# First attention of a two-block network: sums of the query and key products' inputs on VectorE instead of GpSimd

## The chip, the cores and the metric

One core of a Trainium2 chip runs the whole program in one launch. The metric is device time in microseconds (us) of that core; lower is better. TensorE (PE) multiplies, VectorE (DVE), ScalarE (ACT) and GpSimd (POOL) work on elements, SyncE (SP), ACT and POOL issue transfers (DMAs).

## The reference

The input is one sequence of 512 tokens of 1024 channels, float32. The first block is a conformer-like mixer with a SwiGLU network and a final RMS norm. The second has two layers: a "fox" attention layer (16 heads of 64, with a forget gate) and a differential attention layer, each followed by a layer norm and a gated network with a convolution of width 3. What the change touches is the start of the fox attention:

```python
def _fox_attention(x, w_in, b_f, w_out):
    proj = x @ w_in                                  # 1024 -> 3*1024 + 16
    q = _heads(proj[..., :d], FOX_HEADS, HEAD_DIM)
    k = _heads(proj[..., d:2 * d], FOX_HEADS, HEAD_DIM)
    v = _heads(proj[..., 2 * d:3 * d], FOX_HEADS, HEAD_DIM)
    f_logit = proj[..., 3 * d:] + b_f
    c = jnp.cumsum(jax.nn.log_sigmoid(f_logit), axis=1)
    ...                                              # causal softmax(q k^T / 8 + c_q - c_k) v, then @ w_out
```

## The kernel before

Each float32 operand is split into a rounded high part and a low part (`split`, L182: ScalarE copies the high part, L183; VectorE subtracts it from the source for the low part, L185, or GpSimd does where it is asked to). A product is three matmuls, high x high, high x low and low x high (`mm3`, L433 to L438). The activations stand transposed in SBUF as `xh` and `xl`, eight blocks of 128 channels by 512 tokens. Weights come in pieces of 128x1024: SyncE loads a raw tile, ScalarE and VectorE convert it to `wh` and `wl` (`_convert`), four pieces are held at most and two are made ahead of use.

The fox layer (`fox`, L1112) begins while the last product of the network before it (`dn`) ends. VectorE adds that to the residual (L848), GpSimd makes the row's scale (a power, `rs_r`, through the helper `pool`, L176), VectorE scales the row tile (L357), TensorE transposes it (L337, tiles `pt`), and ScalarE and VectorE split it into `xh` and `xl`. This is done for four row tiles of 128 tokens. The value product `ta` (`t_phase`, L1149) starts on the first two row tiles; its two halves of 512 channels are evacuated from PSUM to `va` by `split`. Then come the small forget-gate product `pf` and the query and key products.

Query and key products use a scheme of seven block products instead of eight (`fast_chunk`, L493; PSUM tiles `c1`, `c2`). The weights' combinations are made from loaded blocks: an accumulating transfer on GpSimd's queue (L274, `raw<-raw`) and two GpSimd additions (L277, L278, also `raw<-raw`). The activations' combinations are made once, by `sums` (L465). `xh`+`xl` is taken as four quarters (channel half by token half) of 128x1024 each, then five sums and differences of them, `z`, in two buffers by turns, and each is split into high and low parts: into new tiles (`g1`, `g6`, `g7`) or in place over two quarters of `xh` and `xl`. `sums` is a generator. Its first step (four quarters and two of the five) is traced at the fifth channel block of the value product's first half, together with a spill of the residual X to DRAM; three further steps follow in the second half at blocks 1, 3 and 5, inside `behind(1)`, which orders ScalarE's and VectorE's instructions of the step behind the conversion made last; the rest is traced after the forget gate's chain:

```python
if k == 4 and not half:
    self.spill()
    ...
    next(sums)
elif half and k in (1, 3, 5):
    with self.behind(1):
        next(sums)
```

GpSimd's queue also carries, in this stretch, up to five paced steps: after a conversion a copy of one column of `wh` (L150, `paced`) and then an accumulating transfer of 704 KB for the next network's weights (L152), as well as the load of the forget gate's weights (L1153) and the store of its sums (L1172).

The order of instructions on each engine is set when the program is built: a list scheduler takes, for each engine, the ready instruction that was traced first, by its own model of time, except where a stretch is pinned (`manual_schedule`) or an order is asked for (`issue_after`). Each engine then runs its list in order. The two networks' own sums (`wide`, L788) use the same function with GpSimd and are not touched.

Of the kernel before, what the change touches and what calls it, by code (L numbers as in the profile page):

```python
# [99 lines left out]
class Net:  # L100
# [73 lines left out]
    def pool(self, *args, **kw):  # L174

        self.pooled = self.nc.gpsimd.tensor_tensor(*args, **kw)  # L176
        return self.pooled
# [284 lines left out]
                self.f_tile(ps, self.piece())  # L462
            evac(c, *pss)

    def sums(self, g, new, tmp, zs):  # L465


        A, B = slice(0, 4), slice(4, 8)
        t, u = slice(0, 256), slice(256, 512)
        here = lambda k, q: (self.xh[:, k, q], self.xl[:, k, q])  # L470
        gp = self.pool
        for x, (k, q) in zip(tmp, ((A, t), (A, u), (B, t), (B, u))):
            h, l = here(k, q)
            gp(x, h.bitcast(F32), l.bitcast(F32), op=ALU.add)
        b11, b12, b21, b22 = tmp
        ops = ((b11, b22, ALU.add), (b11, b12, ALU.add), (b21, b22, ALU.add), (b21, b11, ALU.subtract), (b12, b22, ALU.subtract))
        n, z = len(zs), {}

        def add(m):
            if m < len(ops):  # L480
                z[m] = zs[m % n]()
                x, y, op = ops[m]
                gp(z[m], x, y, op=op)

        for m in range(n):
            add(m)
        g.update({2: here(A, t), 5: here(B, u), 1: new(1), 6: new(6), 7: new(7), 4: here(B, t), 3: here(A, u)})
        for m, i in enumerate((1, 6, 7, 4, 3)):
            yield
            self.split(*g[i], z[m])  # L490
            add(m + n)
# [620 lines left out]
    def fox(self):  # L1112
        nc, tc, a = self.nc, self.tc, self.a
        with ExitStack() as es:
            pool = lambda name, bufs=1: es.enter_context(tc.tile_pool(name=name, bufs=bufs))
            self.more = pool("more")
            one = pool("fox")
# [14 lines left out]

            self.fz = two
            sums, g = None, {}

            def lhs_v(k, half):
                nonlocal sums
                if k == 4 and not half:
                    self.spill()
                    f32 = lambda tag, c: two.tile([P, c], F32, name="sum", tag=tag)[:, :1024].rearrange("p (a b) -> p a b", b=256)  # L1140
                    sums = self.sums(g, self.places(one), [f32(tag, 1024) for tag in ("qh", "qh", "kh", "kh")], [partial(f32, "p", 1280)] * 2)
                    next(sums)
                elif half and k in (1, 3, 5):
                    with self.behind(1):
                        next(sums)
                return self.xh[:, k, :], self.xl[:, k, :]

            with self.mixing(1, 5):
                self.t_phase(KD, lhs_v, v_out, tail=2, head=4)  # L1149
# [40 lines left out]
            def scores(u):  # L1190
                j, e = divmod(u, 2)
                p = two.tile([P, 1280], F32, name="p", tag="p")
                for qb in range(NT):
                    n = (qb + 1) * P
                    pq = p[:, po_[qb]:po_[qb] + n]
                    sc = self.qk(qb, e, qs[j], ks[j], ib, mb)
                    nm = self.sm.tile([P, 1], F32, name="nm", tag="nm")
                    sc = sc[:, :n]
                    nc.vector.tensor_tensor_reduce(sc, sc, cbs[j][:, e, :n], 1.0, 3e38, ALU.add, ALU.min, nm)
                    sm = self.sm.tile([P, 1], F32, name="se", tag="se")  # L1200
                    nc.scalar.activation(sc, sc, AF.Exp, bias=nm, scale=-1.0, accum_out=sm)
                    r = self.sm.tile([P, 1], F32, name="re", tag="re")
                    nc.vector.reciprocal(r, sm)
                    nc.vector.tensor_scalar(pq, sc, r, None, op0=ALU.mult)
                return p
# [38 lines left out]
            p = scores(0)  # L1244
            for u in range(16):
# [7 lines left out]
                p = nxt  # L1253
# [8 lines left out]
            g, b = self.row(R_AG), self.row(R_AB)  # L1262
# [300 lines left out]
```

## Time and profile before

| | us |
|---|---|
| Timed runs, median of 3 (lowest, highest) | 1784.56 (1781.68, 1785.53) |
| Profiled execution | 1781.66 |
| its span, first to last instruction | 1779.6 |
| busy in the span: PE / DVE / ACT / POOL | 1673.8 / 1445.4 / 1008.7 / 779.9 |
| mean granted TensorE clock | 0.981 |

All times of the trace count from the first instruction. Busy time is the time in which an engine executed something; a line of a timeline gives the start, the duration, the engine, the line of the kernel, the operation with its output and inputs, and in brackets how long the engine was idle before and which instruction ended that. Where a neighbouring pair is merged, x2 stands behind it. A line number can be that of a helper: L176 is any GpSimd operation through `pool`, L185 the low part of any split. The granted clock is TensorE's, as a share of full speed (2.4 GHz).

### The profile page before, as it was taken

What the parts mean: (1) busy time and instruction counts of PE and PEld (TensorE: products, weight loads), DVE (VectorE), ACT (ScalarE), POOL (GpSimd) and SP (SyncE); (2) the same over time, 40 slices, a digit from 0 to 9 for tenths busy, and PEclk for the clock granted to TensorE, in tenths of its full rate; (3) what the DMA queues carried; (4) which work ended last, traced back from release to release, by engine and by line L of the source; (5) the groups of instructions that cost most, each with busy time, mean ns of one, the idle gap of its engine ahead of it and who ended that gap; (6) DMA issues with size and microseconds to landing.
All of it is one profiled execution on the core that took longest, in us unless ns stands there. A gap on an engine that the chain in (4) does not pass through costs nothing. (4 is left out here: it accounts for less than half of the span.)

```text
span 1779.6 us, 28078 instructions
## 1 busy us (share of the span) xinstructions
PE 1673.8 (94%) x10432; PEld 1485.5 (83%) x10432; DVE 1445.4 (81%) x2198; ACT 1008.7 (57%) x1733; POOL 779.9 (44%) x537
## 2 busy tenths in 40 slices
PE   7977999999999899989999999999888999999996
PEld 6856999998787789879999987787766789999875
DVE  6984676678885789967899899865888679988999
ACT  6662444446552678736666564654667455656563
POOL 2484643330035576217556527334332175465522
PEclk9988999999999999999999999999999999999998
DMA  6469566668967564844566689787443235666552
GB/s 232 169 186 251 152 165 185 180 179 305 342 205 201 140 175 130 222 119 135 136 190 172 176 274 347 222 227 202 113 114 97 79 108 163 179 194 184 190 183 106
DMA packets 106072, 326.05 MB, mean 183 GB/s; under 512 B 9888, under 2 KB 10016, under 8 KB 93904
## 3 DMA queue, kind: packets, MB, share of 16 engines
q1 hardware_dynamic: 73088, 215.53, 35.2%
q0 software_dynamic: 25648, 73.54, 22.1%
q10 hardware_dynamic: 7200, 35.20, 5.5%
q8 instruction: 82, 1.34, 0.3%
q14 instruction: 54, 0.44, 0.1%
HBM read 274.91 MB, written 73.43 MB: 196 GB/s over the span
## 5 line engine op out<-in xcount | busy, mean ns | idle before, releaser
L183 ACT ACTIVATE wh<-raw 128x1024 fp32r<-128x1024 f32 x457 | 450.6, 997 | 405.5 <-PE c L437 94.2
L185 DVE TENSOR_TENSOR wl<-raw,wh 128x1024 fp32r<-128x1024 f32 (+1 forms) x415 | 535.5, 1305 | 139.6 <-ACT wh L183 135.9
L176 POOL TENSOR_TENSOR raw<-raw 128x512 f32<-128x512 f32 x124 | 189.9, 1532 | 255.3 <-DMA raw<-raw 227.9
L436 PE MATMUL c<-xh,wh 128*128 128x256 f32 x992 | 284.2, 287 | 13.3 <-ACT m L519 9.0
L437 PE MATMUL c<-xl,wh 128*128 128x256 f32 x992 | 282.6, 285 | 0.0
L438 PE MATMUL c<-xh,wl 128*128 128x256 f32 x992 | 282.1, 284 | 0.0
L436 PEld LDWEIGHTS c<-xh,wh 128*128 128x128 f32 x992 | 190.8, 192 | 16.1 <-ACT m L519 11.0
L437 PEld LDWEIGHTS c<-xl,wh 128*128 128x128 f32 x992 | 190.9, 192 | 0.1
L438 PEld LDWEIGHTS c<-xh,wl 128*128 128x128 f32 x992 | 190.8, 192 | 0.0
L438 PE MATMUL dn<-wh,hl 128*128 128x512 f32 x462 | 181.7, 394 | 7.7 <-DVE hl L185 7.6
L437 PE MATMUL dn<-wl,hh 128*128 128x512 f32 x462 | 181.8, 394 | 2.5 <-DVE wl L185 2.4
L436 PE MATMUL dn<-wh,hh 128*128 128x512 f32 x462 | 179.1, 394 | 0.1
L436 PE MATMUL fa<-xh,wh 128*128 128x256 f32 (+1 forms) x400 | 133.4, 333 | 1.6 <-ACT wh L183 1.6
L437 PE MATMUL fa<-xl,wh 128*128 128x256 f32 (+1 forms) x400 | 132.8, 332 | 1.2 <-DVE xl L185 1.2
L176 POOL TENSOR_TENSOR wl<-raw,wh 128x1024 fp32r<-128x1024 f32 (+1 forms) x42 | 96.7, 2317 | 84.6 <-ACT wh L183 81.5
L438 PE MATMUL fa<-xh,wl 128*128 128x256 f32 (+1 forms) x400 | 132.6, 331 | 0.5 <-DVE wl L185 0.5
L150 POOL COPY paced<-wh 128x1 f32<-128x1 f32 x48 | 35.8, 745 | 220.1 <-ACT wh L183 220.0
L176 POOL TENSOR_TENSOR rs_r<-rs_t,mhalf 128x1 f32<-128x1 f32 (+1 forms) x40 | 32.3, 809 | 195.1 <-DVE rs_t L326 195.1
L438 PEld LDWEIGHTS dn<-wh,hl 128*128 128x128 f32 x462 | 87.7, 190 | 27.7 <-DVE hl L185 9.7
L176 POOL TENSOR_TENSOR hT<-hT,tv 128x512 f32<-128x512 f32 x44 | 93.2, 2117 | 37.5 <-DVE tv L1004 33.2
L437 PEld LDWEIGHTS dn<-wl,hh 128*128 128x128 f32 x462 | 87.6, 190 | 23.7 <-DVE wl L185 5.7
L436 PEld LDWEIGHTS dn<-wh,hh 128*128 128x128 f32 x462 | 87.8, 190 | 18.7 <-ACT wh L183 0.5
(305 smaller groups left out, 4597.6 us busy)
## 6 DMA issues: line engine op xcount, KB each, us to landing
raw<-in_w_conv_dram SPq DMA_DIRECT2D x36, 1024.0 KB, 4.9
mixed<-in_narrow_dram ACTq DMA_DIRECT2D x48, 704.0 KB, 6.3
raw<-raw POOLq DMA_DIRECT2D x62, 512.0 KB, 5.1
raw<-mixed SPq DMA_DIRECT2D x51, 512.0 KB, 6.0
raw<-in_narrow_dram SPq DMA_DIRECT2D x48, 512.0 KB, 5.5
raw<-in_w_ffn_dram SPq DMA_DIRECT2D x18, 1024.0 KB, 4.8
mixed<-in_narrow_dram POOLq DMA_DIRECT2D x24, 704.0 KB, 10.2
mixed<-mixed POOLq DMA_DIRECT2D x24, 704.0 KB, 9.6
```

Source lines behind the costliest of these rows:

```text
L150: paced = self.nc.gpsimd.tensor_copy(m, self.ready[-1][0][:, 0:1].bitcast(F32))
L176: self.pooled = self.nc.gpsimd.tensor_tensor(*args, **kw)
L183: self.copied = self.nc.scalar.activation(hi, src, AF.Copy)
L185: return self.copied, sub(lo, src, hi.bitcast(F32), op=ALU.subtract)
L436: mm(ps, lh, rh, start=first, stop=False)
L437: mm(ps, lh, rl, start=False, stop=False)
L438: mm(ps, ll, rh, start=False, stop=last)
```

## The change

`sums` takes an engine's two-operand instruction as an optional argument, and the fox layer passes VectorE's. So the four additions of `xh` and `xl` and the five sums and differences, nine instructions of 128x1024 float32, are issued on VectorE. The splits stay on ScalarE and VectorE; the two networks still use GpSimd.

```diff
-    def sums(self, g, new, tmp, zs):
+    def sums(self, g, new, tmp, zs, engine=None):
...
-        gp = self.pool
+        gp = engine or self.pool
         for x, (k, q) in zip(tmp, ((A, t), (A, u), (B, t), (B, u))):
             h, l = here(k, q)
             gp(x, h.bitcast(F32), l.bitcast(F32), op=ALU.add)
...
-                    sums = self.sums(g, self.places(one), [f32(tag, 1024) for tag in ("qh", "qh", "kh", "kh")], [partial(f32, "p", 1280)] * 2)
+                    sums = self.sums(g, self.places(one), [f32(tag, 1024) for tag in ("qh", "qh", "kh", "kh")], [partial(f32, "p", 1280)] * 2, nc.vector.tensor_tensor)
```

## Rows read from the trace of the kernel before

**Rows 1.** The page: busy us of each engine, share of the span, instructions.
```profile
PE 1673.8 (94%) x10432; PEld 1485.5 (83%) x10432; DVE 1445.4 (81%) x2198; ACT 1008.7 (57%) x1733; POOL 779.9 (44%) x537
```

**Rows 2.** Stretches: length, PE, PEld, DVE, ACT, POOL busy, clock, DMA share, GB/s.
```profile
529.00:541.00 12.00, 7.79 (x38) 5.79 (x37) 11.32 (x9) 3.64 (x6) 8.97 (x8) 1.00 0.66 198
541.00:585.00 44.00, 44.00 (x198) 33.80 (x196) 24.84 (x18) 15.57 (x22) 25.91 (x17) 1.00 0.65 162
585.00:590.00 5.00, 0.70 (x5) 0.49 (x5) 5.00 (x5) 2.60 (x4) 2.76 (x2) 1.00 0.65 111
590.00:594.00 4.00, 4.00 (x23) 3.93 (x21) 3.97 (x8) 2.04 (x3) 0.00 (x0) 0.57 0.92 315
...
625.00:760.00 135.00, 132.09 (x946) 117.36 (x944) 121.70 (x347) 102.62 (x238) 67.45 (x46) 1.00 0.65 176
```

**Rows 3.** TensorE's timeline, the four instructions that ended its longer waits.
```profile
533.13 0.50 PE L437 MATMUL ta<-wl,xh 128*128 128x512 f32 x1 [0.94 <-DVE wl L185]
...
540.80 1.07 PE L337 MATMUL pt<-ident,X 128*128 128x128 f32 x8 [3.25 <-DVE X L357]
...
589.51 0.39 PE L436 MATMUL c<-xh,wh 128*128 128x256 f32 x1 [4.29 <-DVE va L185]
...
617.47 0.58 PE L436 MATMUL c<-g1h,wh 128*128 128x256 f32 x1 [2.61 <-ACT wh L183]
```

**Rows 4.** VectorE's timeline, 529 to 591 us.
```profile
529.65 3.42 DVE L185 TENSOR_TENSOR wl<-raw,wh 128x1024 fp32r<-128x1024 f32 x1
...
534.19 2.35 DVE L185 TENSOR_TENSOR wl<-raw,wh 128x1024 fp32r<-128x1024 f32 x2
...
537.28 3.37 DVE L357 SCALAR_TENSOR_TENSOR X<-X,rs_r,row 128x1024 f32<-128x1024 f32 x1 [0.68 <-POOL rs_r L176]
...
548.45 7.21 DVE L185 TENSOR_TENSOR wl<-raw,wh 128x1024 fp32r<-128x1024 f32 x3 [0.65 <-ACT wh L183]
...
560.65 4.03 DVE L185 TENSOR_TENSOR g<-sum,g 128x1024 fp32r<-128x1024 f32 x1
578.51 1.23 DVE L185 TENSOR_TENSOR wl<-raw,wh 128x1024 fp32r<-128x1024 f32 x1 [13.84 <-ACT wh L183]
...
582.02 6.83 DVE L185 TENSOR_TENSOR wl<-raw,wh 128x1024 fp32r<-128x1024 f32 x2
588.78 2.47 DVE L185 TENSOR_TENSOR va<-ta,va 128x512 fp32r<-128x512 f32 x4
```

**Rows 5.** GpSimd's timeline, 529 to 588 us.
```profile
529.39 2.60 POOL L176 TENSOR_TENSOR sum<-xh,xl 128x1024 f32<-128x1024 f32 x1 [0.98 <-PE dn L438]
...
537.24 2.33 POOL L176 TENSOR_TENSOR sum<-xh,xl 128x1024 f32<-128x1024 f32 x1
...
547.70 5.75 POOL L176 TENSOR_TENSOR sum<-sum 128x1024 f32<-128x1024 f32 x2
553.39 1.18 POOL L150 COPY paced<-wh 128x1 f32<-128x1 f32 x1
...
580.86 3.39 POOL L176 TENSOR_TENSOR sum<-sum 128x1024 f32<-128x1024 f32 x1
...
584.99 2.77 POOL L176 TENSOR_TENSOR sum<-sum 128x1024 f32<-128x1024 f32 x1
```

**Rows 6.** Instructions on tile `sum`: ns min/median/max, first and last start.
```profile
L176 POOL TENSOR_TENSOR sum<-sum x5: 2404/2874/3390, 547.7 to 585.0; 128x1024 f32<-128x1024 f32 x5
L176 POOL TENSOR_TENSOR sum<-xh,xl x4: 2333/2389/2595, 529.4 to 545.2; 128x1024 f32<-128x1024 f32 x4
...
L185 DVE TENSOR_TENSOR xl<-sum,xh x2: 1206/1208/1210, 591.8 to 594.0; 128x1024 fp32r<-128x1024 f32 x2
```

**Rows 7.** ScalarE's timeline before the query products.
```profile
577.42 1.06 ACT L183 ACTIVATE wh<-raw 128x1024 fp32r<-128x1024 f32 x1 [17.00 <-DMA raw<-raw]
...
582.84 2.04 ACT L183 ACTIVATE va<-ta 128x512 fp32r<-128x512 f32 x4
```

**Rows 8.** Line L274, 500 to 760 us: accumulating transfers, issue to landing.
```profile
DMA to landing us min/median/max: 5.0/5.6/17.3
```

## The prediction

> **What bounds the kernel now.** I read the page first: TensorE is busy 94% of the span, VectorE 81%, GpSimd 44% [rows 1]. So an edit on VectorE or GpSimd is worth what it does to TensorE's idle time, and I look for that idle time where the nine sums stand. The table of stretches [rows 2] gives it: from 529 to 541 us TensorE works 7.79 of 12.00 us, from 541 to 585 it has no gap, from 585 to 590 it works 0.70 of 5.00 us, and from 590 to 594 it works throughout, at a granted clock of 0.57. In the long attention stretch behind (625 to 760 us) it is busy 132.09 of 135 us and VectorE 121.70; there is nothing in it for this change to gain.
>
> TensorE's own timeline names who ended each gap [rows 3]: 0.94 us for a weight half `wl` (gap a), 3.25 us for VectorE's scaled row tile `X` of L357 (gap b), 4.29 us for the evacuation `va` of the value product (gap c), and later 2.61 us for a converted weight piece (gap f). The reader is to see that a, b and c all wait for VectorE.
>
> Why VectorE was late stands in its timeline, laid beside GpSimd's [rows 4, 5]. The subtraction `wl` at 529.65 took 3.42 us and ended at 533.07; a GpSimd sum ran from 529.39 to 531.99. A pair of such subtractions with no GpSimd sum beside it took 2.35 us (at 534.19), so one takes about 1.2. The scaling at 537.28 took 3.37 us; a GpSimd sum ran from 537.24 to 539.57. The pair at 582.02 took 6.83 us, beside the sums at 580.86 (3.39 us) and 584.99 (2.77 us). Each time the VectorE instruction lasts about its own time plus what was left of the sum: the two engines take turns on such operands. So a sum on GpSimd costs VectorE twice what it would cost there, while VectorE holds what TensorE waits for.
>
> **The change, part by part.**
> *Removed from GpSimd:* nine sums of 128x1024, four of `xh`+`xl` (median 2389 ns) and five of sums (median 2874 ns), 23.9 us [rows 6].
> *Added to VectorE:* the same nine. No row shows this addition on VectorE; the nearest has the same size, the same strided blocks and both inputs in SBUF: `xl<-sum,xh`, 1206 to 1210 ns [rows 6]. I take 1.21 us each, 10.9 us in all. The lower end is the back-to-back price of half the pair at 534.19, 1.18 us; the upper, if a GpSimd instruction runs beside it, the 3.42 us of the blocked `wl`. Few GpSimd instructions are left there to do that, hence the low end.
> *Given back on VectorE:* the stalls behind sums [rows 4]. At 529.65: 3.42 - 1.2 = 2.2 us; at 537.28: 3.37 - 1.2 = 2.2; the three at 548.45: 7.21 - 3.5 = 3.7; at 560.65: 4.03 - 1.2 = 2.8; the pair at 582.02: 6.83 - 2.35 = 4.5. Together 15.4 us against 10.9 added: VectorE is 4.5 us less busy.
>
> The price that matters is that at TensorE's gaps.
> - Gap a: `wl` at 529.65 ends at 530.9 instead of 533.07, before TensorE wants it (533.13 - 0.94 = 532.2). Even with one sum of 1.21 us ahead of it it ends at 532.1. Saved: 0.94 us (0 to 0.94).
> - Gap b: without a sum beside it the scaling ends 2.2 us earlier. Everything behind the `wl` of gap a (the residual additions, ScalarE's square, the scaling) also comes up to 2.2 us earlier, and one or two of the four sums whose inputs exist by then may stand ahead of it, at 1.21 us each. These two I let cancel: 2.2 us (0.7 to 3.25).
> - Gap c: the first query product needs a PSUM buffer that `va` frees. ScalarE delivers its half at 583.4 (the first of four in 2.04 us from 582.84 [rows 7]), but VectorE's half starts at 588.78, behind the pair of 6.83 us. With 2.35 us for the pair and one sum of 1.21 ahead of it, VectorE is through with the pair at 582.0 + 3.56 = 585.6 and with its first `va` at 586.2 (a quarter of 2.47 us), if its input chain doesn't move. TensorE was free at 585.2 (589.51 - 4.29), and gaps a and b bring it there 3.1 us sooner, at 582.1. So the chain has to come sooner as well. It begins with the accumulating transfer of the first query/key block, which ScalarE awaits until 577.42 [rows 7]: 17.3 us to landing where the median is 5.6 [rows 8]. Ahead of it on the same queue are three paced weight transfers of 704 KB, which GpSimd issues from 553.39 on, once its sums of 547.70 are done [rows 5]. With the sums gone, GpSimd's queue (L150, L152, L1153, L274) moves up. By how much it lands earlier no row shows: at most 17.3 - 5.6 = 11.7 us, at the least nothing, and below nothing if the paced transfers collide with the block's own load. I take the length of the two sums ahead of them less the conversions they also wait for: an estimate of 4 us from the 5.75 us of those two [rows 5]. Then `va` is there at 582.2 and gap c closes: 4.3 us saved (0.2 if the landing stays at 577).
> - Clock: after gap c the granted clock is 0.57 for 4.00 us of full work [rows 2], which costs 4.00 x 0.43 = 1.7 us. After the 3.25 us of gap b it stayed at 1.00, so a gap of that size need not lower it. With c closed I count the 1.7 (0 to 1.7).
>
> Three of the five `z` sums stand in a new order: they are traced behind the weight conversion made last on VectorE (the `behind(1)` block), and each needs a `z` buffer that a split frees. The first two of them are ready by 564.7 (the split at 560.65 [rows 4]), and VectorE then has 13.84 us with nothing to do until 578.51, which hides them; the last follows the third split and costs its 1.21 us ahead of the pair, counted above. Queued behind these sums are weight halves and `va`; what hides them from TensorE is that it has converted pieces in hand (no gap from 541 to 585 [rows 2]). If that cover is gone, each sum costs TensorE 1.21 us.
>
> A rule that speaks against the change stands in the Trainium skill, page "Perfetto Trace Analysis", section "Optimizing Scalar/DVE Operations": the two engines share an SBUF read port, so shifting work between them might not help, and with a saturated VectorE work should rather go off it. By that the sum would be about nothing. The trace agrees on the sharing (3.42 us beside a sum, 2.35 for two without one) and not on the conclusion here, since the same sum holds the port for 2.4 to 2.9 us from one side and 1.2 from the other.
>
> Sum: 0.9 + 2.2 + 4.3 + 1.7 = 9.1 us. The profiled execution took 1781.66 us, 2.1 beyond its span, and lies 2.9 below the median of the three timed runs, 1784.56. Its time would become 1772.6; from the median, which I take as the likelier level of the next runs, 1775.5.
>
> **The rivals.**
> 1. *The forecast*, 9.1 us gained: 1775.5. For it: all three gaps end on a VectorE instruction that ran beside a sum.
> 2. *The transfer decides.* The first block still lands at 577; then `va` comes at 586.2 whatever happened before, and TensorE starts the query products there instead of at 589.51. Gained 3.3 us; the idle time before them remains about 4 us and the clock drops all the same: 1781.3. For it: 17.3 us to landing with the DMA engines full. Against: its queue moves up.
> 3. *Given back behind.* TensorE runs into the weight supply instead: gap f shows that the third block already comes 2.61 us late. If the supply to the third block keeps its time, f grows by what was gained and all behind 617 stands where it stood: 1784.6. Against: each load waits for a buffer that a VectorE `wl` frees, and these come sooner too.
> 4. *VectorE's queue.* Program order is only a wish: the sums may be put ahead of what TensorE waits for, from the first on, with none in an idle time. Then they cost 9 x 1.21 = 10.9 us, against 0.94 + 2.2 + 4.3 = 7.4 returned at the gaps: 3.5 us slower, 1788.1. It decides as soon as more than six of the nine (7.4 / 1.21) stand in TensorE's way. Against: TensorE has no gap from 541 to 585, where all but the first two start [rows 2, 5], and VectorE is idle for 13.8 us of that.
>
> **How the numbers follow.** Chances: forecast 0.60, transfer 0.13, given back 0.15, queue 0.12. Time 1775.5. The forecast's own span is 1772 (b wholly closed, and a little of the smaller gaps) to 1780 (c's clock term gone and b at its low end). 0.2% is 3.6 us, about what a measurement here tells from no change: below 1781.0 is faster. That holds nearly all of the forecast and half of the transfer case: 0.66. Within: the given-back case, the rest of the transfer case and a little of the forecast: 0.22. Slower: the rest, 0.12. The range of 1770 to 1786 reaches from 5.5 us below the forecast, for orders that change elsewhere, over the given-back case; it leaves out most of the queue case and the tails.
>
> **What would show it.** Right: VectorE's `wl` and scaling at 1.2 to 1.3 us in the whole stretch, nine sums of 1.2 us in its timeline; GpSimd's paced copies some 5 us sooner; the three gaps of [rows 3] below 1.5 us in all; granted clock 1.00 at the start of the query products. Wrong in a step: a TensorE wait of over 2 us for `X` or `va` (order or transfer), a wait for the accumulating transfer that still ends 36 us after gap b (transfer), or gap f beyond 5 us (given back). Wrong as a whole: TensorE's first query product no earlier than about 588 us, or new idle time in the attention stretch, which I hold to be untouched.

## The result, and the profile after

The changed kernel took 1773.7 us (median of 4 runs, 1772.77 to 1777.4), the kernel before beside it 1785.05 us (4 runs, 1781.68 to 1785.81). The ratio is 0.9945, with a 95% interval of 0.9918 to 0.9972: 9.8 us faster, give or take 4.8. The forecast was 1775.5.

The profiled execution of the changed kernel took 1772.77 us, its span is 1770.8. Engine totals of its page, then TensorE's timeline with the four places that answer to [rows 3]; it runs 0.63 us behind that of before when this stage begins (first product on `ta` at 529.71 instead of 529.08).

```profile
PE 1668.4 (94%) x10432; PEld 1481.3 (84%) x10432; DVE 1446.9 (82%) x2207; ACT 1010.3 (57%) x1733; POOL 785.3 (44%) x528
```

```profile
538.05 1.06 PE L337 MATMUL pt<-ident,X 128*128 128x128 f32 x8 [0.64 <-DVE X L357]
556.81 0.50 PE L436 MATMUL ta<-wh,xh 128*128 128x512 f32 x1 [0.61 <-DVE va L185]
582.90 0.28 PE L436 MATMUL c<-xh,wh 128*128 128x256 f32 x1
587.43 0.39 PE L436 MATMUL c<-xh,wh 128*128 128x256 f32 x1 [1.49 <-ACT m L519]
607.44 0.39 PE L436 MATMUL c<-g1h,wh 128*128 128x256 f32 x1 [0.49 <-ACT wh L183]
608.70 0.38 PE L438 MATMUL c<-g1h,wl 128*128 128x256 f32 x1 [0.45 <-DVE wl L185]
```

Of the four waits of [rows 3], the first and the third are gone (no bracket stands behind 582.90), the second fell from 3.25 to 0.64 us and the fourth from 2.61 to 0.49, with 0.45 more behind it. Two waits are larger or new: 0.61 us at 556.81 for `va`, and 1.49 us at 587.43 for ScalarE's `m`, where before had 0.42.

The stretches answer to [rows 2]; TensorE's clock is 1.00 where the query products begin, instead of 0.57:

```profile
529.00:541.00 12.00, 11.32 (x56) 8.87 (x55) 11.46 (x14) 5.56 (x10) 4.69 (x7) 1.00 0.83 225
585.00:594.00 9.00, 7.26 (x58) 6.85 (x58) 8.22 (x10) 6.29 (x9) 3.09 (x3) 1.00 0.40 69
617.00:752.00 135.00, 129.08 (x913) 114.64 (x912) 118.12 (x335) 98.51 (x228) 65.13 (x44) 0.99 0.65 172
```

VectorE's timeline (to [rows 4]), GpSimd's (to [rows 5]), the sums (to [rows 6]), and when ScalarE gets the first block of query weights (to [rows 7]), with the landing of the accumulating transfers in 500 to 760 us (to [rows 8]):

```profile
530.28 1.22 DVE L185 TENSOR_TENSOR wl<-raw,wh 128x1024 fp32r<-128x1024 f32 x1
534.95 1.21 DVE L474 TENSOR_TENSOR sum<-xh,xl 128x1024 f32<-128x1024 f32 x1
536.62 1.28 DVE L357 SCALAR_TENSOR_TENSOR X<-X,rs_r,row 128x1024 f32<-128x1024 f32 x1 [0.46 <-POOL rs_r L176]
...
570.91 1.23 DVE L185 TENSOR_TENSOR wl<-raw,wh 128x1024 fp32r<-128x1024 f32 x1 [10.03 <-ACT wh L183]
...
575.54 2.35 DVE L185 TENSOR_TENSOR wl<-raw,wh 128x1024 fp32r<-128x1024 f32 x2
577.81 2.48 DVE L185 TENSOR_TENSOR va<-ta,va 128x512 fp32r<-128x512 f32 x4
583.81 2.64 DVE L1166 SCALAR_TENSOR_TENSOR fe<-fz 16x512 f32<-16x512 f32 x1 [1.18 <-ACT fz L1164]
```

```profile
546.75 1.23 POOL L150 COPY paced<-wh 128x1 f32<-128x1 f32 x1 [10.17 <-ACT wh L183]
562.45 1.21 POOL L274 DMA_DIRECT2D raw<-raw  x1 [10.31 <-issue]
```

```profile
L483 DVE TENSOR_TENSOR sum<-sum x5: 1214/1219/1226, 547.9 to 574.4; 128x1024 f32<-128x1024 f32 x5
L474 DVE TENSOR_TENSOR sum<-xh,xl x4: 1211/1214/1216, 534.9 to 542.5; 128x1024 f32<-128x1024 f32 x4
```

```profile
569.81 1.06 ACT L183 ACTIVATE wh<-raw 128x1024 fp32r<-128x1024 f32 x1 [12.45 <-DMA raw<-raw]
```

```profile
DMA to landing us min/median/max: 5.0/5.3/7.2
```

The reader is to see three things. The nine sums take 1.21 to 1.23 us on VectorE, and `wl`, the scaling and the pair of `wl` have their undisturbed lengths (1.22, 1.28 and 2.35 us instead of 3.42, 3.37 and 6.83). GpSimd's paced copy comes at 546.75 instead of 553.39. And the first block is at ScalarE at 569.81 instead of 577.42: its transfer, issued at 562.45 (32.7 us after the first `ta`; 30.8 in before), now lands within 7.2 us at most instead of 17.3.

The table below follows the same stretch of TensorE through all kernels of the study, in one profiled execution each. Its times are worked out from TensorE's timelines: from the first product on `ta` to the last of the gate's `pf`, from there to the first query product `c`, from there to the first score product `sc`, and the sum of the three. All are taken between starts, so `pf` to `c` is 0.23 or 0.24 where TensorE does not wait. "Block" is when ScalarE takes the first block, counted from the first `ta`. The ratio to before is that of the timed runs.

| kernel | `ta` to `pf` | `pf` to `c` | `c` to `sc` | sum | block | ratio [95%] |
|---|---|---|---|---|---|---|
| before | 55.7 | 4.69 | 28.55 | 89.0 | 48.3 | 1 |
| after | 53.0 | 0.23 | 24.88 | 78.1 | 40.1 | 0.9945 [0.9918, 0.9972] |
| e1, only the 4 input sums moved | 52.1 | 0.23 | 27.68 | 80.0 | 40.0 | 0.9952 [0.9930, 0.9975] |
| e2, only the 5 others moved | 58.3 | 0.24 | 25.75 | 84.3 | 44.4 | 0.9961 [0.9939, 0.9984] |
| e3, after + dummy sums | 63.9 | 0.24 | 25.54 | 89.7 | 49.1 | 1.0008 [0.9991, 1.0025] |
| e4, after + dummy fills | 52.1 | 0.24 | 25.20 | 77.6 | 39.4 | 0.9948 [0.9933, 0.9964] |
| e5, before, no paced transfers | 58.2 | 0.24 | 25.26 | 83.7 | 36.8 | 1.0102 [1.0072, 1.0132] |
| e6, after, block held back | 52.1 | 2.37 | 30.25 | 84.7 | 46.9 | 0.9989 [0.9972, 1.0007] |
| e7, all networks' sums moved | 52.1 | 0.23 | 26.19 | 78.6 | 38.4 | 1.0067 [1.0043, 1.0092] |
| e8, after + block's additions | 52.1 | 0.23 | 25.85 | 78.2 | 38.1 | 0.9943 [0.9924, 0.9961] |
| e9, before, transfers put off | 55.8 | 0.24 | 25.99 | 82.0 | 41.2 | 0.9989 [0.9977, 1.0000] |
| e10, after, transfers put off | 52.2 | 0.23 | 25.32 | 77.7 | 30.7 | 0.9945 [0.9927, 0.9963] |

### The profile page after: what moved, and what is told of

It reads as the page before. It is cut to its first block, busy times and chain, and to the rows that moved or that the text cites. A ratio compares the mean times of both kernels' runs of the same rounds, so it can differ in the third digit from the quotient of the medians.

```text
span 1770.8 us, 28075 instructions
## 1 busy us (share of the span) xinstructions
PE 1668.4 (94%) x10432; PEld 1481.3 (84%) x10432; DVE 1446.9 (82%) x2207; ACT 1010.3 (57%) x1733; POOL 785.3 (44%) x528
## 5 line engine op out<-in xcount | busy, mean ns | idle before, releaser
L176 POOL TENSOR_TENSOR raw<-raw 128x512 f32<-128x512 f32 x124 | 184.4, 1487 | 247.7 <-DMA raw<-raw 203.2
L176 POOL TENSOR_TENSOR hT<-hT,tv 128x512 f32<-128x512 f32 x44 | 100.1, 2274 | 36.3 <-DVE tv L1004 29.0
L274 POOL DMA_DIRECT2D raw<-raw x62 | 74.2, 1196 | 70.9 <-DVE wl L185 21.0
## 6 DMA issues: line engine op xcount, KB each, us to landing
mixed<-in_narrow_dram POOLq DMA_DIRECT2D x24, 704.0 KB, 10.2
```

Of the source, the lines that this page charges most:

```text
L274: self.nc.gpsimd.dma_start(out=raw[:, 0:4:2, :], in_=raw[:, 1:4:2, :], accum_op=ALU.add)
```

## The experiments

Two causes were open. The *port*: a VectorE instruction that runs beside a GpSimd sum takes what is left of that sum's time too. The *landing*: GpSimd's queue moves up, and the first block comes sooner. Both vanish together in the change.

**e1 and e2: one half of the change each.** Against the changed kernel, e1 gives the five sums of sums back to GpSimd:

```diff
-                gp(z[m], x, y, op=op)
+                self.pool(z[m], x, y, op=op)
```

> Only the four additions of xh and xl stay on VectorE; the five z sums go back to GpSimd. Theory P (a sum on GpSimd holds up VectorE instructions that run beside it, and only those): gaps a and b stay closed (at most 1 us together against 0.94 + 3.25 before), the weight subtractions beside the z sums last over 2 us again, and gap c (the query products waiting for va) comes back with 2 us or more; about 3 us faster than before, near 1782, when the block lands as late as before. Theory Q (GpSimd's queue and the accumulating transfer behind it decide): the paced transfers and the first block come earlier because four sums are gone from the queue, ScalarE gets the block by 573 instead of 577, and gap c stays under 1.5 us; near 1777.

e2 gives back the four additions of `xh` and `xl` instead:

```diff
-            gp(x, h.bitcast(F32), l.bitcast(F32), op=ALU.add)
+            self.pool(x, h.bitcast(F32), l.bitcast(F32), op=ALU.add)
```

> The counterpart: the five z sums on VectorE, the four additions of xh and xl back on GpSimd. Theory P: gaps a and b return as before (0.94 and 3.25 us, the subtraction and the scaling at 3.4 us each), gap c is gone and the clock at the query products is 1.00; 5 to 7 us faster than before, near 1779. Theory Q: the paced transfers still stand behind the four additions, the block lands within 2 us of before's time, and gap c keeps 2 us or more; at most 3 us faster.

e1 took 1772.68 us (7 runs) and e2 1775.29 us (10 runs), before beside them 1782.58 us (26 runs). By the ratios that is 8.6 and 7.0 us gained, give or take 4 each; e1 alone can't be told from the whole change. TensorE's timeline of e2 has the waits a and b back; VectorE's of e1, and ScalarE's of e1 below it, show why gap c closes there:

```profile
534.01 0.50 PE L437 MATMUL ta<-wl,xh 128*128 128x512 f32 x1 [0.94 <-DVE wl L185]
541.68 1.94 PE L337 MATMUL pt<-ident,X 128*128 128x128 f32 x8 [3.23 <-DVE X L357]
```

```profile
573.61 6.89 DVE L185 TENSOR_TENSOR wl<-raw,wh 128x1024 fp32r<-128x1024 f32 x2
580.43 2.47 DVE L185 TENSOR_TENSOR va<-ta,va 128x512 fp32r<-128x512 f32 x4
```

```profile
569.02 1.06 ACT L183 ACTIVATE wh<-raw 128x1024 fp32r<-128x1024 f32 x1 [12.33 <-DMA raw<-raw]
```

In e1 the pair of residuals is held beside GpSimd's sums as long as ever, 6.89 us, and still the first query product follows `pf` without a wait, since the block came 8.3 us sooner. So a and b belong to the four input sums, as predicted, and gap c needs no free port: theory P, which had c return in e1 with 2 us or more, fails there. Each half moves the block, by 8.3 us (e1) and 3.9 (e2), and each closes c. That is why the halves don't add in the stretch, where they give 9.0 and 4.7 us beside 10.9 for both; in the runs the intervals are too wide to tell 15.6 from 9.8.

**e3 and e4: the load put back on GpSimd, with and without the port.** Both are the changed kernel; GpSimd gets, for each of the nine sums on VectorE, an addition of two blocks of 128x896 into an unused place (e3), or a one-column copy and two fills of 128x1024 (e4, 18 fills in all, 18.9 us busy). Neither is part of the result.

```diff
+                    self.pool(self.extra, x[:, :, :224], y[:, :, :224], op=op)
```

```diff
+        c = self.nc.gpsimd.tensor_copy(m, x[:, 0, 0:1])
+        with self.tc.issue_after(c.ins):
+            for _ in range(2):
+                self.nc.gpsimd.memset(self.extra, 0.0)
```

> The changed kernel, and GpSimd does each of the nine sums once more (128x896 instead of 128x1024) into a part of a tile that nothing has used yet; nobody waits for these results. Theory P: the stalls come back although VectorE does the sums, the subtractions and the scaling beside a dummy last 2.5 to 3.5 us, gap b is over 2 us; at or above the time of before, 1784 to 1792, since VectorE has the sums and the stalls. Theory Q: only GpSimd's queue is later, so a and b stay closed and gap c opens by the delay of the first block; 1776 to 1780.

> The changed kernel, and GpSimd copies one column of each sum's input and then fills 128x1024 with zeros twice, nine times: it is busy for as long as with the sums, but reads almost nothing from SBUF. Theory P: no VectorE subtraction lasts over 1.5 us beside a fill, a and b stay closed, and the time stays within 3 us of the changed kernel, 1772 to 1777. Theory Q: a queue that is as full as before brings the first block as late as before (577), gap c opens by 2 to 4 us; 1777 to 1782. A third possibility, that any GpSimd work beside VectorE slows it, writes too: as the dummy sums, 1784 or more.

e3 took 1783.4 us and loses the whole gain; e4 took 1772.77 us and loses nothing. The sums on VectorE, of e3 and then of e4, four fills of e4 and the pair of residuals beside them, and TensorE's longest wait in e3:

```profile
L485 DVE TENSOR_TENSOR sum<-sum x5: 1211/1225/3143, 551.2 to 583.1; 128x1024 f32<-128x1024 f32 x5
...
L474 DVE TENSOR_TENSOR sum<-xh,xl x4: 1214/2024/3148, 535.9 to 545.1; 128x1024 f32<-128x1024 f32 x4
```

```profile
L492 DVE TENSOR_TENSOR sum<-sum x5: 1214/1217/1226, 546.4 to 575.2; 128x1024 f32<-128x1024 f32 x5
L481 DVE TENSOR_TENSOR sum<-xh,xl x4: 1211/1214/1217, 536.4 to 544.0; 128x1024 f32<-128x1024 f32 x4
```

```profile
574.00 4.00 POOL L470 MEMSET pT<- 128x1024 f32 x4
```

```profile
576.32 2.35 DVE L185 TENSOR_TENSOR wl<-raw,wh 128x1024 fp32r<-128x1024 f32 x2
```

```profile
563.52 0.79 PE L436 MATMUL ta<-wh,xh 128*128 128x512 f32 x1 [7.72 <-DVE va L185]
```

From 529 to 594 us GpSimd is as busy in e4 (37.86 us) as in before (37.64), VectorE's sums keep 1.21 to 1.23 us, and the pair of residuals keeps its 2.35 us beside four fills; beside additions the sums take up to 3.15. So it is not GpSimd's busy time that costs but the operands it reads. This is as the Trainium skill has it (page "SBUF — State Buffer", section "Who interferes with whom"): a VectorE instruction with two SBUF inputs contends with a GpSimd instruction that reads SBUF, not with one that only writes. Two limits: the fills of e4 run from 547.62 us on, behind the four input sums, and the additions of e3 from 541.96 on, behind the scaling, which keeps its 1.28 us; so neither repeats what stood at gaps a and b, and e3's wait for `X` is 1.59 us where over 2 was expected. And neither tells port from landing: in e4 the block comes as early as in the changed kernel (39.4 us), and in e3 the additions stand in GpSimd's queue ahead of its transfer, so that it is late as well (issued 39.3 us after the first `ta`, taken at 49.1).

**e5 and e6: the landing moved, in either direction.** e5 is the kernel before with the five paced transfers taken out of the value product and made up for in the product behind the attention (the expectation speaks of leaving out the copies; the edit moves the transfers themselves):

```diff
-            with self.mixing(1, 5):
+            with self.mixing(0, 5):
...
-            with self.mixing(1):
+            with self.mixing(2):
```

> The kernel before, all 36 sums still on GpSimd; one thing is changed: in the transposes ahead of the first attention the transfers are mixed in without the paced copies, so that the first block of the query weights is fetched earlier. Theory A (the wait ahead of the first query product is a matter of when the block lands): the block reaches ScalarE by about 572 us instead of 577.4, that gap of 4.29 us falls below 1.5 us although VectorE's sums and stalls stay as before, the gaps of 0.94 and 3.25 us stay, and the time falls by 4 to 6 us, to about 1778 us. Theory B (it is a matter of the port: the pair of residuals that takes 6.83 us beside GpSimd's sums): the pair still takes over 6 us, the gap keeps 3 us or more, and the time falls by at most 1.5 us.

e6 is the changed kernel with the first block's accumulating transfer behind a one-column copy and ten fills. The copy waits for the block's raw tile, so that two of the three paced transfers behind it come late too (at 557.92 and 560.31 us; 549.06 and 551.33 in the changed kernel):

```diff
+                last = self.nc.gpsimd.tensor_copy(m, raw[:, 1, 0:1])
+                for _ in range(10):
+                    with self.tc.issue_after(last.ins):
+                        last = self.nc.gpsimd.memset(self.extra, 0.0)
```

> The changed kernel, with the accumulating transfer of the first block of the query weights held back by some 10 us of fills on GpSimd (fills of an unused tile, no part of the result), so that the block lands at about 577 us as in the kernel before. Theory A (landing decides): the gap ahead of the first query product comes back with 3 to 4.5 us, the clock falls behind it, and the time is 1777 to 1781 us. Theory B (the port decides): the pair of residuals takes 2.4 us instead of 6.8, which makes up for the late landing; the gap stays under 1.5 us and the time at or below 1776 us.

e5 took 1799.06 us, 1.0% slower than before, where either theory expected faster: a miss of the experiment's design. In the stretch itself the block is taken 11.5 us sooner, c is gone and 5.3 us are saved, as theory A had it; but the two `wl` of the pair were not held there either (1.87 and 1.23 us), so e5 does not tell the two theories apart. The transfers come back from 721 us on, at the attention's end; TensorE waits there for a stored half of the keys, 4.72 us, where before had no wait of that kind, and the stretch from the last `c` to the first `fa`, the first product of the next network, grows from 80.2 to 89.0 us:

```profile
753.51 0.55 PE L1107 MATMUL sc<-kh,qh 128*128 128x256 f32 x1 [4.72 <-DMA kh<-kl]
```

In this execution another 10.5 us go behind that `fa`, and 2.9 ahead of the stretch, which no run here explains.

e6 took 1780.82 us (before beside it 1781.73): by the ratio 2.0 us are left of the gain (-1.2 to 5.0) with the block 6.8 us later (46.9 instead of 40.1), although the two `wl` of the former pair take 1.22 and 1.23 us. TensorE's timeline, ScalarE's and VectorE's:

```profile
584.45 0.39 PE L446 MATMUL c<-xh,wh 128*128 128x256 f32 x1 [1.97 <-DVE va L186]
...
614.36 0.39 PE L446 MATMUL c<-g1h,wh 128*128 128x256 f32 x1 [3.13 <-ACT wh L184]
```

```profile
576.83 1.06 ACT L184 ACTIVATE wh<-raw 128x1024 fp32r<-128x1024 f32 x1 [19.20 <-DMA raw<-raw]
```

```profile
583.71 2.48 DVE L186 TENSOR_TENSOR va<-ta,va 128x512 fp32r<-128x512 f32 x4
```

Gap c came back with 1.97 us, between the two expectations (3 to 4.5, under 1.5): VectorE starts on `va` 6.9 us after ScalarE has the block, instead of 11.4 in before, which makes up for part of the delay. More is lost behind: the later blocks come late too, gap f is 3.13 us, and the stretch from `c` to `sc` is 30.25 us, the longest of all. Even so the sum, 84.7 us, is 4.3 below before's.

**e9 and e10: the landing moved with less harm.** Three of the five paced transfers, those that stand just ahead of the block on GpSimd's queue, are put off into the attention loop, in before (e9) and in the changed kernel (e10):

```diff
-            with self.mixing(1, 5):
+            with self.mixing(1, 2):
...
+                if 7 <= u < 10:
+                    self.steps.pop(0)()
```

> The kernel before, its 36 sums on GpSimd, with three of the paced transfers that stand just ahead of the first block's accumulating transfer on GpSimd's queue (issued at 554 to 557 us there) put off into the attention loop (its turns 7 to 9, near 700 us, where DMA share was 0.36). Theory A (the gap ahead of the first query product is a matter of when the block lands): the accumulating transfer lands in 5 to 7 us instead of 17.3, ScalarE has the block by 570 us, that gap falls below 1 us with the pair of residuals still held beside GpSimd's sums, the gaps of 0.94 and 3.25 us stay, the first score product comes 4 to 6 us sooner after the first transpose product than before's 89.0 us, and the time is 4 to 7 us below before (1775 to 1778 us). Theory B (the port alone): the stretch of 89.0 us shortens by less than 2 us and the time by less than 2 us.

> The changed kernel with the same three paced transfers put off into the attention loop. Theory A (the landing has nothing more to give there, since no gap of TensorE waits for the first block any longer): the stretch from the first transpose product to the first score product stays within 1.5 us of 78.1 us and the time within 2 us of the changed kernel's (1771.5 to 1775.5 us). Theory B (the later blocks too are still held by these transfers, the wait of 0.94 us at the first g1h product with them): the stretch falls to 74 to 76 us and the time to 1769 to 1771 us.

e9 took 1780.31 us (11 runs; before 1781.81 in 17), e10 1773.25 us (6 runs). Of e9, the waits of TensorE, then VectorE's pair and ScalarE's block:

```profile
535.39 0.50 PE L437 MATMUL ta<-wl,xh 128*128 128x512 f32 x1 [0.93 <-DVE wl L185]
543.06 1.06 PE L337 MATMUL pt<-ident,X 128*128 128x128 f32 x8 [3.25 <-DVE X L357]
587.34 0.28 PE L436 MATMUL c<-xh,wh 128*128 128x256 f32 x1
758.87 0.39 PE L1107 MATMUL sc<-kh,qh 128*128 128x256 f32 x1 [2.48 <-DVE pT L185]
```

```profile
577.19 6.87 DVE L185 TENSOR_TENSOR wl<-raw,wh 128x1024 fp32r<-128x1024 f32 x2
583.98 2.47 DVE L185 TENSOR_TENSOR va<-ta,va 128x512 fp32r<-128x512 f32 x4
```

```profile
572.60 1.06 ACT L183 ACTIVATE wh<-raw 128x1024 fp32r<-128x1024 f32 x1 [9.91 <-DMA raw<-raw]
```

With every sum still on GpSimd, a and b stand as before, the pair is held for 6.87 us, and c is gone. The transfer landed in 10.2 us, not in the 5 to 7 expected, and ScalarE has the block at 572.60, not by 570, yet the stretch shortened by 7.0 us, more than the 4 to 6. The time did not follow: the runs show 2.0 us by the ratio (0.0 to 4.1). In the profiled execution, 2.3 us had gone before the stretch began, and 3.7 go in the attention's end (last `c` to first `fa` 83.9 us instead of 80.2; the wait for `pT` at 758.87 is 2.48 us, 0.88 in before). e10 has 83.8 there and the kernels that move no paced transfer have 77.4 to 81.8, so the transfers put off are the likely price; but e10 keeps the changed kernel's time with them, and that they cost e9 its gain is not shown. So theory A holds for the stretch, and its forecast for the whole time failed. e10 has the block 9.4 us sooner again than the changed kernel and gains nothing by it (77.7 us against 78.1): what the landing could give there, the change has taken.

**e7 and e8: more of the same change.** e7 passes VectorE in the networks' call of `sums` as well (27 more sums), e8 lets VectorE make GpSimd's two additions for each of the first two blocks.

```diff
-                for _ in self.sums(b, new, tmp, zs):
+                for _ in self.sums(b, new, tmp, zs, self.nc.vector.tensor_tensor):
```

```diff
+                gp = self.nc.vector.tensor_tensor
```

> The changed kernel, with the other 27 sums, those ahead of the three networks' products, on VectorE too. Theory A (a sum costs only where VectorE is what TensorE waits for): no gap of TensorE over 1 us stands on VectorE where those sums run, so the time stays within 2 us of the changed kernel's (1772 to 1776 us), and VectorE's busy time changes by less than 15 us. Theory B (every sum taken from GpSimd is worth what the first nine were, about 1.1 us each): 1745 us or less. Theory C (VectorE, busy 82%, becomes the bound there): gaps on VectorE appear in those stages and the time is over 1778 us.

> The changed kernel, with GpSimd's two additions for each of the first two blocks of query weights made by VectorE as well. Theory A (what is left of the port's cost there is the 1.49 us gap at 587 us, behind an operation of VectorE held up beside two such additions): that gap closes, the first block is ready about 2 us sooner, and the time is 1 to 3 us below the changed kernel's. Theory B (VectorE is the busier engine there, 68% in 585 to 594 us by the trace, and four more operations of 1.2 us delay the evictions): no gain, or up to 3 us slower, with a new gap on VectorE.

e7 took 1792.01 us, 0.7% slower than before: theory C. TensorE's timeline has a new long wait on VectorE where a network's first products start (the two of the later networks shown; the first has 2.37 us at 241.97, the changed kernel no wait for `g1l` there):

```profile
859.57 0.58 PE L437 MATMUL p<-g1l,wh 128*128 128x256 f32 x1 [7.03 <-DVE g1l L185]
...
1485.55 0.58 PE L437 MATMUL p<-g1l,wh 128*128 128x256 f32 x1 [8.82 <-DVE g1l L185]
```

and the granted clock falls behind them (0.86 as the mean of 1450 to 1500 us; 1.00 before those waits, in 1400 to 1450). For e8, VectorE is busier in 585 to 594 us than the 68% that its expectation names: 8.22 of 9.00 us by the changed kernel's row. e8 took 1773.4 us, the same as the changed kernel (1773.7): the block came the expected 2.0 us sooner and the wait for `m` fell from 1.49 to 1.04 us, but the one for the third block at `g1h` rose from 0.49 to 2.42, and the stretch kept its 78.2 us. Nothing was gained, as theory B had it, though for ScalarE's `wh` and not for VectorE. No kernel of the study beats the changed one by more than its interval.

## Why the prediction was right

**Gaps a and b** (0.9 and 2.2 us forecast). Both went nearly as worked out: `wl` and the scaling take their undisturbed 1.22 and 1.28 us, and one sum, not two, was placed ahead of the scaling (534.95). Gap a gave its 0.94, gap b 2.6 instead of 2.2. e2, with the four input sums back on GpSimd, has both waits again to within 0.02 us: this step is shown.

**Gap c** (4.3 us). It closed, as forecast, and the reason needed correction in its weight. The prediction held that both were wanted, the shorter pair and an earlier chain. e1 and e9 close it with the pair still held for 6.9 us; e6, with a free port and the block late, keeps 1.97 us. The lines shown give each cause its size. From ScalarE's taking the block to VectorE's start on `va` it is 11.4 us with the pair held (before 588.78 - 577.42, e1 580.43 - 569.02, e9 583.98 - 572.60) and 8.0 without (after, 577.81 - 569.81). So the free port is worth 3.4 us at this place, about what the prediction took (`va` from 589.51 to 586.2, 3.3 us), and the landing 8.2. TensorE, through with `pf` 2.8 us sooner after the first `ta` because a and b are closed, needed 4.3 + 2.8 = 7.1 us: the landing alone gives that, the port alone does not. The landing was the mis-sized term: 4 us estimated, 8.2 measured (40.1 instead of 48.3 us after the first `ta`). The estimate was taken from the length of the sums ahead of the paced transfers. These transfers are issued 5.5 to 6.6 us sooner, and so are mostly out of the way when the block's own starts, which then takes at most 7.2 us instead of 17.3. e9 shows it with the sums left on GpSimd: issued 30.8 us after the first `ta` as in before (562.20 - 531.35 against 559.92 - 529.08), it lands in 10.2 us.

**Clock** (1.7 us). The granted clock is 1.00 behind the first query product, as forecast. But one ground given for the size of gaps was weak: "a gap of that size need not lower it" rested on gap b of one execution. The same wait left the clock at 1.00 in e9 (3.25 us) and at 0.50, the 1.2 GHz level, for the 4 us behind it in e2 (3.23 us) and e5 (3.62 us): the transposes behind it took 1.94 us (e2) instead of 1.06 for eight. In e6 a wait of 1.97 us was followed by a mean of 0.64 in 584 to 588 us. What decides between the two levels these traces don't show. The drop costs about 2.5 us (`ta` to `pf` 58.2 and 58.3 us in e5 and e2, 55.7 and 55.8 in before and e9). So the kernel before may lose that at gap b in some executions, though its profile does not have it; it was in no term of the sum.

**What was in no term.** Gap f shrank by 1.67 us, where the *given back* rival had it grow. But the other kernels with an early first block have 1.24 to 2.42 us at the same place (e4 1.24, e10 1.90, e8 2.42), so this is no settled effect of the change. Against it stand the 0.61 us at 556.81, where a sum was placed between two pairs of `va` (554.94), and the 1.07 us more for `m`, behind the forget gate's `fe`, which took 2.64 us beside GpSimd's additions to a block (0.67 in before). The sum had neither. But e4, e8 and e10, with the same sums on VectorE, have less than 0.4 at the first place and 1.04 at the second, and e9, with the sums on GpSimd, has 1.05 there: neither is shown to be a price of the change.

**The sum.** 9.1 us were forecast to the start of the attention. The stretch shortened by 10.9: 2.8 to the last `pf`, 4.46 at c, 3.67 behind. By the runs the whole time is 9.8 us less. In the stretch, the landing alone (e9) gives 7.0 and the rest with most of the landing taken back (e6) 4.3, together 11.3 beside 10.9. The runs are too coarse to bear this out: there e9 and e6 are each 2.0 us below before, 4 together beside 9.8, with intervals of 2 to 5 us either way. So the split between the two causes is shown for the stretch, in one execution of each kernel, and not for the time of the runs.

**The rivals.** *The transfer decides* did not happen, since the block did not stay late, but its mechanism is real: where the block is made to come late, gap c is back and what is left of the gain is not clear of noise (e6). Its price, 3.3 us still gained, lies within e6's interval (-1.2 to 5.0). *VectorE's queue* did not happen: one sum stood ahead of the scaling of gap b, one between two pairs of `va`, and 0.61 us came of the second. e7 shows the same mechanism as real where VectorE has less idle time than the sums take: in 1450 to 1500 us it is busy 44.00 of 50 us in the changed kernel, and nine sums take 10.9. There TensorE waits 7 to 9 us at a network's start. *Given back behind* did not happen in the runs. In the profiled execution, the attention is 4.7 us longer than before's (first `sc` to last `c`, 112.6 against 107.9), which "untouched" had excluded:

```profile
640.82 1.53 PE L1227 MATMUL po<-pT,va 128*128 128x512 f32 x8 [2.32 <-DVE re L1203]
...
678.56 0.52 PE L1215 MATMUL ptp<-ident,p 128*128 128x128 f32 x3 [2.48 <-DVE p L1204]
```

The two waits were 1.25 and 0.27 us in before. The ten other variants (107.7 to 109.9 us) do not repeat it. It is taken as one execution's; why that execution had it was not tried.

**VectorE** was to be 4.5 us less busy. For the same work, first `ta` to first `sc`, it was busy 60.70 us of 529 to 618 before and 59.04 of 529 to 608 after: 1.7 less. Some stalls stayed, beside GpSimd's additions to the blocks (`fe` 2.64 us, a split of 2.31 at 572.05).

**What stays open.** How the 9.8 us of the runs divide between landing, port and the clock at gap b, where e6 and e9 give only 2.0 us each; and what sets the clock's level behind a wait of 3.2 us.

## What to carry to other kernels

Price an operation moved between GpSimd and VectorE at the instruction that the other engine is waiting to start, not at its busy time: 23.9 us of sums on GpSimd cost VectorE some 12.6 us of stalls (10.9 us of sums came to it, and it was 1.7 us less busy), and 18.9 us of fills cost nothing that the runs show. Look for idle time of the receiving engine ahead of what waits: with eight of the nine sums done, VectorE still had 10.0 us with nothing to do before the block came (570.91), while 27 more sums elsewhere made the kernel 0.7% slower than before. And follow the queue: in this stretch more came from the transfers behind the sums than from the sums (e9: 7.0 of 10.9 us), since those transfers were out of the way when a block on TensorE's path wanted to land.

## What the runs showed of the hardware

The two-input addition that takes 2.4 to 2.9 us on GpSimd (medians of before) takes 1.21 to 1.23 us on VectorE, and up to 3.15 us beside a GpSimd addition (e3). Beside GpSimd fills VectorE's subtractions keep their length (a pair 2.35 us, e4). An accumulating transfer of 512 KB landed in 17.3 us behind three transfers of 704 KB (before), in at most 7.2 us when those were issued 5.5 to 6.6 us sooner (after), and in 10.2 (e9) and 5.0 us (e10) without them. Waits of 3.23 and 3.25 us of TensorE left the granted clock at 0.50 in one execution (e2) and at 1.00 in two others (before, e9). One conclusion drawn from a rule was not borne out: that work shifted between these two engines might not help (Trainium skill, page "Perfetto Trace Analysis", section "Optimizing Scalar/DVE Operations") holds for e7's 27 sums, which made the kernel 0.7% slower than before, and not for these nine.
